# A diagonal of reciprocal roots in place of scaling and transposes, in the norm ahead of a feed-forward part

## The chip, the cores and the metric

The kernel runs on one core of a Trainium2 chip. The time is that of one execution on the device, in microseconds (us); what is given for a kernel is the median of its runs. Each engine has a queue of its own, which it works through in order, and waits in it for semaphores: TensorE (PE, with PEld for its weight loads), VectorE (DVE), ScalarE (ACT), GpSimd (POOL) and SyncE (SP), which only issues DMAs here.

## What is computed

One layer of a latent generator, with 1024 positions of 1024 channels in fp32 (and 256 context positions, which end before the part that matters here): a modulated norm, an input projection, three mixing groups (Fourier, attention, gated DeltaNet), an output projection with a gate, and a feed-forward part with squared ReLU. The change lies in the second norm, between the two residual additions:

```python
def _rms(x, g):
    xf = x.astype(jnp.float32)
    y = xf * lax.rsqrt(jnp.mean(xf * xf, axis=-1, keepdims=True) + EPS)
    return (y * g.astype(jnp.float32)).astype(x.dtype)
...
    x = x + g1 * _mix_out(P, o_att, o_dn, lp['w_out'], lp['o_norm'])
    x = x + g2 * _mlp(_rms(x, lp['norm2']) * (1 + sc2) + sh2, lp['w_ff1'], lp['w_ff2'])
```

The feed-forward products contract over channels, so the normed rows are needed transposed, with channels on the partitions. There a channel's `norm2 * (1 + sc2)` and `sh2` are one number for each partition.

## The kernel before

The whole program is unrolled, and every tile of 128x128 or 128x512 is an instruction of its own. A scheduler sets the order on each engine when the program is built, by a model of how long instructions take and by priorities: code under `tc.high_priority(n)` is preferred by n places. So a change of a few lines can shift instructions of other code too. In what follows "L1480" is line 1480.

Products of fp32 accuracy are made by three products each, of high and low parts: `mm3` (L235 to L238) multiplies high by high, high by low and low by high, in the type fp32r. `mm` (L233) is a single product, in the type of its operands; with plain fp32 operands it is an fp32 product. `tp` (L241) is a transpose on PE, a product with the identity in transpose mode. All three write to PSUM banks (`ba`, `bk`). `act` (L220) is an ACT operation, so all ACT work carries that line. `split` (L1488 to L1490) cuts a tile into a high part (a cast, by ACT or DVE) and a low part (a subtraction, by DVE or POOL).

In front of the change stands the output projection (L1528 to L1554): four passes over 256 output columns, in each eight row tiles q. A tile's product goes through DVE (L1544, times the gate) and POOL (L1545, added to `ACC[q]`, the residual row tile of 128 x 1024). In the last pass `ACC[q]` is complete, and under the priority OFN = 1000 follow:

- `rms_ff(q)` (L1470): ACT squares the row tile with a running sum (two instructions that write `bk_78`), POOL works out the mean (L1474, L1475) and the reciprocal root (L1476, a power), one number for each row;
- a store of the row tile to DRAM (L1549), needed later for the second residual addition;
- after q = 3, `h2_first` (L1492): the first half, rows 0 to 511. `norm_ff(0)` (L1478 to L1480) scales four row tiles by their roots on DVE, 128 x 1024 each. Then for each block k of 128 channels `h2_T` (L1482) makes four transposes into one bank of a ring of three (`bk_76`, `bk_77`, `bk_79`), and ACT evicts the bank with the scale and the shift of that block's channels. DVE casts the high part (L1489); the low part goes to POOL for odd k and to DVE for even k.

The second half, rows 512 to 1023, is scaled with `norm_ff(1)` (priority OFN2 = 0) into the same four tiles ACC[0] to ACC[3], and `h2_second` (L1575, priority OFN3 = 400) makes the same transposes and evictions. It also needs differences with the first half: `joined` (L1580) puts the first half's high and low parts back together in a bank by two products with an identity (L1582, L233), and DVE subtracts (L1576). The feed-forward's first product is a Strassen-Winograd scheme of seven products (named 11, 12, s1, s2, s4, s3, 22), so it takes sums and differences of weights as well: `w1_prep` (L1517) makes the weights' sums on POOL (L1523, 128 x 512) in a ring `shr` of three buffers, which the first half's blocks use too; ACT casts the high part, DVE subtracts the low part (L1490). `ff1` (L1605) runs the products.

Buffers: `g1r` are the two buffers of the output projection's gate, `mrowb` two of the modulation rows, 256 columns each; `slot` are the 16 half tiles of `ACC`, reused after the norm for `t1`, `tr_` and the ring `ur` of the feed-forward's results.

Of the kernel before, what the change touches and what calls it, by code (L numbers as in the profile page):

```python
# [14 lines left out]
ALU = mybir.AluOpType  # L15
AX = mybir.AxisListType

P = 128
# [173 lines left out]
def body(tc, t, out):  # L192
# [3 lines left out]
    with ctx:  # L196
# [14 lines left out]
        V, G, T, Y, SC = nc.vector, nc.gpsimd, nc.tensor, nc.sync, nc.scalar  # L211
# [20 lines left out]
        def mm(o, l, r, start, stop):  # L232
            pe(T.matmul(o, l, r, start=start, stop=stop))  # L233
# [6 lines left out]
        def tp(o, i):  # L240
            pe(T.transpose(o, i, C["ident"]))  # L241
# [7 lines left out]
        C = {k: cstb[a >= 256]()[:, a % 256 if a < 256 else a - 256 : b if a < 256 else b - 256] for k, (a, b) in CST.items()}  # L249
# [3 lines left out]
        mrowb = [buf(256) for _ in range(2)]  # L253
# [1216 lines left out]
        def rms_ff(q):  # L1470
# [4 lines left out]
            G.tensor_scalar(st[:, 0:1], st[:, 0:1], 1.0 / D, EPS, op0=ALU.mult, op1=ALU.add)  # L1475
            G.tensor_tensor(st[:, 1:2], st[:, 0:1], neghalf[:, 0:1], op=ALU.pow)  # L1476

        def norm_ff(half):  # L1478
            for n in range(half * 4, half * 4 + 4):
                V.tensor_scalar(ACC[n - half * 4][:, :], ACC[n][:, :], rsb[n]()[:, 1:2], None, op0=ALU.mult)  # L1480

        def h2_T(k, hf):  # L1482
            b = tr2.next()
            for q in range(4):
                tp(b[:, q * P : (q + 1) * P], ACC[q][:, k * P : (k + 1) * P])
            act(hf, b, AF.Identity, scale=a2()[:, k : k + 1], bias=s2()[:, k : k + 1])

        def split(i, hi, lo, eng, heng=None):  # L1488
# [3 lines left out]
        def h2_first():  # L1492
            norm_ff(0)
            for k in range(KT):
                hf = shr.next()()
                h2_T(k, hf)
                hb = B11 if k < 4 else B21
                split(hf, hb[0]()[:, k % 4], hb[1]()[:, k % 4], G if k % 2 else V, V.tensor_copy)

# [57 lines left out]
            b.free()  # L1557
        with tc.high_priority(OFN2):
            norm_ff(1)
        for b in g1r + otb + catF + catD:  # L1560
            b.free()


# [6 lines left out]
            hpc += [x for pr_ in prs for x in pr_]  # L1570
            HB[nm] = [(x(), y()) for x, y in prs]
        slot = [view(b, z * 512, 512) for b in accb for z in range(2)]
        ur = Ring(slot[14:16] + slot[0:8:2] + slot[1:8:2] + slot[8:14])

        def h2_second():  # L1575
            sub = lambda o, i, x: V.tensor_tensor(o, i, x, op=ALU.subtract)  # L1576
            t1, tr_ = [x() for x in slot[8:12]], Ring([x() for x in slot[12:14]])

            def joined(nm, k):
                b = tr2.next()  # L1580
                for z in range(2):
                    mm(b, idb(), HB[nm][k][z], z == 0, z == 1)  # L1582
                return b

            for k in range(4):
                h2_T(k, t1[k])
                sub(t1[k], t1[k], joined("11", k))
                split(t1[k], *HB["t1"][k], V)
            for k in range(4):
                h22 = tr_.next()  # L1590
                h2_T(k + 4, h22)
# [65 lines left out]

        with tc.high_priority(OFN3):
            h2_second()
        ORDER = ("11", "12", "s1", "s2", "s4", "s3", "22")  # L1660
        for j in range(2):
            for nm in ORDER[0:2]:
# [161 lines left out]
```

## Time and profile before

| | us |
|---|---|
| median of 3 runs | 1450.36 |
| lowest and highest run | 1446.81, 1450.94 |
| the profiled execution, its own time | 1444.78 |
| its span, first to last instruction | 1443.0 |

What lies around the span is 1.78 us. The core's mean granted clock in the profiled execution was 0.985 of full speed.

In the profile a line of a timeline gives the start and length of instructions of one kind in a row, the engine, the source line, operation, tiles and shapes, their number, and in brackets the engine's idle time in front and what ended it. A line of the windows gives, for each engine, the busy time in that stretch of the span and the number of instructions; PEclk is TensorE's granted clock as a share of full speed. A group's line gives after the bar its busy time in us and the mean of one in ns, and after the second bar idle time in front of it. Tile names leave the buffer's number out: `bk` is any of the `bk_` banks, `fbase` any fp32 buffer of a large pool, `rbase` any fp32r buffer, `z1c` and `z2b` buffers of two more pools.

### The profile page before, as it was taken

What the parts mean: (1) busy time and instruction counts of PE and PEld (TensorE: products, weight loads), DVE (VectorE), ACT (ScalarE), POOL (GpSimd) and SP (SyncE); (2) the same over time, 40 slices, a digit from 0 to 9 for tenths busy, and PEclk for the clock granted to TensorE, in tenths of its full rate; (3) what the DMA queues carried; (4) which work ended last, traced back from release to release, by engine and by line L of the source; (5) the groups of instructions that cost most, each with busy time, mean ns of one, the idle gap of its engine ahead of it and who ended that gap; (6) DMA issues with size and microseconds to landing.
All of it is one profiled execution on the core that took longest, in us unless ns stands there. A gap on an engine that the chain in (4) does not pass through costs nothing.

```text
span 1443.0 us, 28992 instructions
## 1 busy us (share of the span) xinstructions
PE 1384.1 (96%) x11462; PEld 1116.0 (77%) x11462; DVE 987.1 (68%) x1697; ACT 703.4 (49%) x1239; POOL 645.7 (45%) x749
## 2 busy tenths in 40 slices
PE   5899989999999999989899899999999999999997
PEld 1677988867777777777799677888888888888886
DVE  0774679966778777787533987655556676776884
ACT  1742423235777777777313755555455543433331
POOL 2663667763546464484433634434443000000872
PEclk8999999989999999999999999999999999999999
DMA  9873133260000010142322225444446998766641
GB/s 330 327 253 125 45 99 80 63 154 17 9 25 10 10 40 2 37 138 66 105 91 107 84 81 174 162 148 151 135 137 225 323 387 261 237 233 218 197 154 59
DMA packets 143832, 198.46 MB, mean 138 GB/s; under 512 B 51549, under 2 KB 86991, under 8 KB 143439
## 3 DMA queue, kind: packets, MB, share of 16 engines
q1 hardware_dynamic: 142992, 195.91, 41.5%
q8 instruction: 90, 1.47, 0.4%
q10 hardware_dynamic: 703, 0.69, 0.1%
q14 instruction: 47, 0.39, 0.1%
HBM read 150.62 MB, written 45.94 MB: 136 GB/s over the span
## 4 chain that ended last, share of the span: by engine, by line
PE 48%; DVE 3%; DMA 2%; POOL 2%; issue 1%; ACT 0%; SPq 0%; DVEq 0%; POOLq 0%; ACTq 0%
PE bk L237 8%; PE bk L238 8%; PE bk L236 8%; PE ba L236 7%; PE ba L237 7%; PE ba L238 7%; PE bk L233 1%; DMA fbase<-la 1%; DMA la<-fbase 0%; DVE z1b L1355 0%; DMA fbase<-w_out 0%; POOL rbase L1490 0%; DMA fbase<-x 0%; PE bk L241 0%; DVE rbase L1018 0%
## 5 line engine op out<-in xcount | busy, mean ns | idle before, releaser
L220 ACT ACTIVATE rbase<-fbase 128x512 fp32r<-128x512 f32 (+3 forms) x255 | 171.4, 685 | 86.3 <-PE bk L237 55.7
L220 ACT ACTIVATE fbase<-bk 128x512 f32<-128x512 f32 (+3 forms) x224 | 124.9, 561 | 150.6 <-PE bk L233 94.1
L233 PE MATMUL bk<-rbase 128*128 128x256 f32 (+2 forms) x984 | 172.9, 310 | 4.4 <-ACT fbase L220 2.5
L233 PEld LDWEIGHTS bk<-rbase 128*128 128x128 f32 (+1 forms) x984 | 131.7, 174 | 34.1 <-ACT fbase L220 3.3
L220 ACT ACTIVATE z1c<-fbase 128x512 fp32r<-128x512 f32 (+1 forms) x120 | 76.7, 653 | 139.1 <-DMA fbase<-w_ff 53.3
L233 PE MATMUL ba<-rbase 128*65 128x512 f32 (+4 forms) x576 | 138.2, 342 | 5.6 <-DVE rbase L1018 4.3
L1523 POOL TENSOR_TENSOR fbase<-fbase 128x512 f32<-128x512 f32 x64 | 87.4, 1366 | 114.7 <-DVE z1c L1490 89.8
L220 ACT ACTIVATE fbase<-fbase 128x512 f32<-128x512 f32 (+4 forms) x148 | 96.0, 659 | 83.7 <-POOL fbase L1646 27.2
L1728 POOL TENSOR_TENSOR z2c<-z2c,fbase 128x512 f32<-128x512 f32 x16 | 31.1, 1967 | 204.5 <-ACT z2c L220 128.6
L994 DVE TENSOR_REDUCE fbase<-ba 128x1 f32<-128x512 f32 (+1 forms) x192 | 106.4, 594 | 21.3 <-PE ba L233 20.1
L220 ACT ACTIVATE rbase<-z1d 128x1024 fp32r<-128x1024 f32 x61 | 63.0, 1054 | 101.4 <-PE bk L237 86.8
L1490 DVE TENSOR_TENSOR z1c<-fbase,z1c 128x512 fp32r<-128x512 f32 x112 | 91.7, 823 | 24.2 <-ACT z1c L220 20.4
L1490 DVE TENSOR_TENSOR rbase<-z1d,rbase 128x1024 fp32r<-128x1024 f32 x61 | 84.9, 1408 | 32.0 <-ACT rbase L220 31.9
L1018 POOL TENSOR_TENSOR rbase<-fbase,rbase 128x512 fp32r<-128x512 f32 x56 | 72.1, 1287 | 67.5 <-ACT rbase L220 60.0
L236 PE MATMUL bk<-rbase 128*128 128x512 f32 x256 | 99.6, 389 | 0.0
L237 PE MATMUL bk<-rbase 128*128 128x512 f32 x256 | 99.6, 389 | 0.0
L238 PE MATMUL bk<-rbase 128*128 128x512 f32 x256 | 99.6, 389 | 0.0
L1018 DVE TENSOR_TENSOR rbase<-fbase,rbase 128x512 fp32r<-128x512 f32 x104 | 80.1, 770 | 24.4 <-ACT rbase L220 24.0
L1490 DVE TENSOR_TENSOR rbase<-fbase,rbase 128x1024 fp32r<-128x1024 f32 (+1 forms) x65 | 81.1, 1266 | 21.9 <-ACT rbase L220 21.6
L233 PEld LDWEIGHTS ba<-rbase 128*65 128x65 f32 (+1 forms) x576 | 76.1, 154 | 23.6 <-DVE rbase L1018 5.4
L237 PE MATMUL ba<-rbase 128*128 128x512 f32 x192 | 74.7, 389 | 0.0
L238 PE MATMUL ba<-rbase 128*128 128x512 f32 x192 | 74.7, 389 | 0.0
(350 smaller groups left out, 3773.1 us busy)
## 6 DMA issues: line engine op xcount, KB each, us to landing
fbase<-w_ff SPq DMA_DIRECT2D x70, 512.0 KB
u<-fbase SPq DMA_DIRECT2D x112, 256.0 KB
z2a<-w_mod SPq DMA_DIRECT2D x36, 512.0 KB
z1d<-w_ff SPq DMA_DIRECT2D x34, 512.0 KB
z1d<-u SPq DMA_DIRECT2D x33, 512.0 KB
fbase<-u SPq DMA_DIRECT2D x23, 512.0 KB
fbase<-w_in SPq DMA_DIRECT2D x16, 512.0 KB
fbase<-x SPq DMA_DIRECT2D x14, 512.0 KB
```

The source lines that it names most:

```text
L220: return SC.activation(o, i, f, **k)
L233: pe(T.matmul(o, l, r, start=start, stop=stop))
L236: pe(T.matmul(o, lh, rh, start=start, stop=False))
L237: pe(T.matmul(o, lh, rl, start=False, stop=False))
L238: pe(T.matmul(o, ll, rh, start=False, stop=stop))
L994: V.tensor_reduce(st4[:, z : z + 1], b, AX.X, ALU.max)
L1018: (G if k2 in GP and not any(a <= n < b for a, b in NGP) else V).tensor_tensor(hl[:, :, 1], p, f32(hl[:, :, 0]), op=ALU.subtract)
L1490: eng.tensor_tensor(lo, i, f32(hi), op=ALU.subtract)
L1523: G.tensor_tensor(w[nm], w[a], w[b], op=op)
L1728: G.tensor_tensor(c, c, G2[cs_.start // 512], op=ALU.mult)
```

## The change

Four views of 128 x 128 are cut out of `g1r[0]` and `mrowb[0]`. `norm_ff` no longer scales row tiles: it writes, for each row tile, the identity times the column of reciprocal roots, a diagonal matrix. `h2_T` no longer transposes: it multiplies the untouched slice of `ACC` (as the operand that is held, so that it comes out transposed) by that diagonal, in one fp32 product. So transposing and scaling are one operation. The row tiles are no longer overwritten, and the second half is read where it lies. `g1r` is released after `h2_second` instead of before it, and the slots of `t1`, `tr_` and `ur` change, since ACC[4] to ACC[7] now stay in use longer.

```diff
+        dgb = [view(b, z * P, P) for b in (g1r[0], mrowb[0]) for z in range(2)]
+
         def norm_ff(half):
             for n in range(half * 4, half * 4 + 4):
-                V.tensor_scalar(ACC[n - half * 4][:, :], ACC[n][:, :], rsb[n]()[:, 1:2], None, op0=ALU.mult)
-
-        def h2_T(k, hf):
+                V.tensor_scalar(dgb[n % 4](), C["ident"], rsb[n]()[:, 1:2], None, op0=ALU.mult)
+
+        def h2_T(half, k, hf):
             b = tr2.next()
             for q in range(4):
-                tp(b[:, q * P : (q + 1) * P], ACC[q][:, k * P : (k + 1) * P])
+                mm(b[:, q * P : (q + 1) * P], ACC[half * 4 + q][:, k * P : (k + 1) * P], dgb[q](), True, True)
             act(hf, b, AF.Identity, scale=a2()[:, k : k + 1], bias=s2()[:, k : k + 1])
...
-        for b in g1r + otb + catF + catD:
+        for b in otb + catF + catD:
             b.free()
...
-        ur = Ring(slot[14:16] + slot[0:8:2] + slot[1:8:2] + slot[8:14])
+        ur = Ring(slot[6:16] + slot[0:6])
...
-            t1, tr_ = [x() for x in slot[8:12]], Ring([x() for x in slot[12:14]])
+            t1, tr_ = [x() for x in slot[0:4]], Ring([x() for x in slot[4:6]])
...
         with tc.high_priority(OFN3):
             h2_second()
+        for b in g1r:
+            b.free()
```

The calls of `h2_T` pass the half. From `norm_ff` on, the changed kernel's lines are two higher than before's: POOL's weight sum is L1525 there, the low part's subtraction L1492, the subtractions of the second half L1578, the scaling L1482; the products stand on L233 and no longer on L241.

The scheduler also puts other instructions elsewhere. On ACT, at the change from the first half to the second, the last evictions of the first half read `bk_76` and `bk_77`, the `z1c` rows are casts of weights, and the first row that reads `bk_79` behind them evicts block 0 of the second half. In before:

```order
L220 ACTIVATE fbase<-bk_76,fbase 128x512
L220 ACTIVATE fbase<-bk_77,fbase 128x512
L220 ACTIVATE z1c<-fbase 128x512
L220 ACTIVATE fbase<-ba_73 128x512
L220 ACTIVATE z1c<-fbase 128x512 x3
L220 ACTIVATE fbase<-bk_79,fbase 128x512
```

And in the changed kernel, from the last eviction of `bk_77` on:

```order
L220 ACTIVATE fbase<-bk_77,fbase 128x512
L220 ACTIVATE z1c<-fbase 128x512 x2
L220 ACTIVATE bk_78,fbase<-fbase 128x512
L220 ACTIVATE fbase<-ba_73 128x512
L220 ACTIVATE z1c<-fbase 128x512 x3
L220 ACTIVATE fbase<-fbase 128x512 x2
L220 ACTIVATE z1c<-fbase 128x512 x3
L220 ACTIVATE fbase<-bk_79,fbase 128x512
```

Four casts stand ahead of that eviction in before, eight in the changed kernel, and the last three of them moved there past it.

On POOL, the last reciprocal roots (L1474 to L1476) lie among sums of weights and low parts of the first half. In before:

```order
L1474 TENSOR_TENSOR fbase<-fbase 128x1
L1523 TENSOR_TENSOR fbase<-fbase 128x512
L1475 TENSOR_SCALAR fbase<-fbase 128x1
L1490 TENSOR_TENSOR rbase<-fbase,rbase 128x512
L1476 TENSOR_TENSOR fbase<-fbase 128x1
L1523 TENSOR_TENSOR fbase<-fbase 128x512 x7
```

And in the changed kernel, where the last root is the last L1476:

```order
L1475 TENSOR_SCALAR fbase<-fbase 128x1
L1525 TENSOR_TENSOR fbase<-fbase 128x512
L1476 TENSOR_TENSOR fbase<-fbase 128x1
L1492 TENSOR_TENSOR rbase<-fbase,rbase 128x512
L1547 TENSOR_TENSOR fbase<-fbase 128x256
L1525 TENSOR_TENSOR fbase<-fbase 128x512
L1474 TENSOR_TENSOR fbase<-fbase 128x1
L1525 TENSOR_TENSOR fbase<-fbase 128x512
L1475 TENSOR_SCALAR fbase<-fbase 128x1
L1525 TENSOR_TENSOR fbase<-fbase 128x512
L1476 TENSOR_TENSOR fbase<-fbase 128x1
L1525 TENSOR_TENSOR fbase<-fbase 128x512 x3
```

Of the eight sums one stands ahead of the last root in before, and five do in the changed kernel; three are left behind it.

On DVE, where the second half's first subtractions (reading a `bk_` bank) begin, `z1c` rows are low parts of weight sums and `z2b` rows low parts of the second half. In before:

```order
L1480 TENSOR_SCALAR fbase<-fbase 128x1024
L1490 TENSOR_TENSOR z1c<-fbase,z1c 128x512 x2
L1631 TENSOR_TENSOR fbase<-ba_74,fbase 128x512
L1490 TENSOR_TENSOR z1c<-fbase,z1c 128x512
L1576 TENSOR_TENSOR fbase<-fbase,bk_76 128x512
L1576 TENSOR_TENSOR fbase<-fbase,bk_79 128x512
L1490 TENSOR_TENSOR z1c<-fbase,z1c 128x512
L1490 TENSOR_TENSOR z2b<-fbase,z2b 128x512
L1490 TENSOR_TENSOR z1c<-fbase,z1c 128x512
```

And in the changed kernel:

```order
L1492 TENSOR_TENSOR z1c<-fbase,z1c 128x512 x3
L1633 TENSOR_TENSOR fbase<-ba_74,fbase 128x512
L1482 TENSOR_SCALAR fbase<-fbase 128x128
L1492 TENSOR_TENSOR z1c<-fbase,z1c 128x512 x3
L1578 TENSOR_TENSOR fbase<-fbase,bk_76 128x512
L1578 TENSOR_TENSOR fbase<-fbase,bk_79 128x512
L1492 TENSOR_TENSOR z2b<-fbase,z2b 128x512 x2
```

The low parts of weight sums that lay between and behind the first subtractions now lie ahead of them, so that from the first subtraction to the second row of L1638 (L1640 in the changed kernel) DVE has 32 instructions where it had 35.

More of the change, by code (lines that the diff above doesn't have):

```diff
@@ L1495, in h2_first @@
                 hf = shr.next()()
-                h2_T(k, hf)
+                h2_T(0, k, hf)
                 hb = B11 if k < 4 else B21
@@ L1585, in h2_second @@
             for k in range(4):
-                h2_T(k, t1[k])
+                h2_T(1, k, t1[k])
                 sub(t1[k], t1[k], joined("11", k))
@@ L1590, in h2_second @@
                 h22 = tr_.next()
-                h2_T(k + 4, h22)
+                h2_T(1, k + 4, h22)
                 sub(t1[k], h22, t1[k])
```

## The prediction

> **What bounds the kernel now.** I read the profile page first, for the busy shares.
>
> ```profile
> span 1443.0 us, 28992 instructions
> PE 1384.1 (96%) x11462; PEld 1116.0 (77%) x11462; DVE 987.1 (68%) x1697; ACT 703.4 (49%) x1239; POOL 645.7 (45%) x749
> ```
>
> TensorE (PE) is busy for 96% of the span, so the change is read from the stretch in which its instructions run. Next came the busy time of each engine by windows, from the end of the output projection to the end of the feed-forward products.
>
> ```profile
> core 0: us, PE busy (x) PEld busy (x) DVE busy (x) ACT busy (x) POOL busy (x), PEclk, DMA share, GB/s
> 770.00:800.00 30.00, 30.00 (x246) 29.14 (x245) 17.39 (x28) 17.26 (x39) 16.48 (x30) 1.00 0.39 148
> 800.00:805.00 5.00, 5.00 (x23) 4.00 (x23) 4.33 (x5) 2.07 (x4) 4.83 (x6) 1.00 0.52 170
> 805.00:810.00 5.00, 4.19 (x21) 3.08 (x21) 4.37 (x4) 0.74 (x2) 4.83 (x6) 1.00 0.00 0
> 810.00:815.00 5.00, 2.67 (x11) 1.57 (x11) 3.96 (x4) 3.82 (x7) 4.15 (x4) 1.00 0.01 3
> 815.00:820.00 5.00, 4.20 (x15) 3.45 (x16) 4.96 (x6) 5.00 (x10) 4.71 (x3) 0.66 0.26 72
> 820.00:825.00 5.00, 3.81 (x23) 2.69 (x22) 5.00 (x9) 4.80 (x9) 0.00 (x0) 1.00 0.56 190
> 825.00:840.00 15.00, 15.00 (x66) 12.03 (x65) 13.03 (x23) 9.84 (x18) 0.00 (x0) 1.00 0.05 18
> 840.00:850.00 10.00, 9.43 (x39) 6.76 (x38) 8.86 (x16) 4.99 (x9) 3.27 (x2) 1.00 0.18 55
> 850.00:1425.00 575.00, 575.00 (x2508) 469.53 (x2507) 388.37 (x426) 261.71 (x369) 185.60 (x119) 1.00 0.60 201
> ```
>
> From 770 to 805 PE never idles; from 805 to 850 it idles 0.81 + 2.33 + 0.80 + 1.19 + 0.57 = 5.7 us; from 850 to 1425 again not at all. Work added to PE in the first or last of these stretches is paid in full; work added in the middle one can replace waiting. The waits of PE between 800 and 850 name the causes (in us, times, longest):
>
> ```profile
> PE bk L241 <- DVE fbase L1576: 2.6, 3, 1.4
> PE bk L233 <- ACT fbase L220: 1.8, 1, 1.8
> PE bk L241 <- DVE fbase L1480: 0.8, 1, 0.8
> PE ba L236 <- DVE fbase L1638: 0.6, 1, 0.6
> ```
>
> Only one wait, 0.8 us, is for the scaling (L1480) that the change replaces. The rest is for the eviction of the first block of the second half (L220) and for the subtractions behind it (L1576). PE's timeline shows where each falls:
>
> ```profile
> 798.25 0.60 PE L241 MATMUL bk<-fbase 128*128 128x128 f32 x4
> 809.86 0.44 PE L241 MATMUL bk<-fbase 128*128 128x128 f32 x2 [0.81 <-DVE fbase L1480]
> 811.54 0.40 PE L238 MATMUL bk<-rbase,z1c 128*128 128x512 f32 x1
> 813.69 0.73 PE L233 MATMUL bk<-rbase 128*128 128x512 f32 x2 [1.76 <-ACT fbase L220]
> 815.80 1.01 PE L241 MATMUL bk<-fbase 128*128 128x128 f32 x4 [1.38 <-DVE fbase L1576]
> 820.99 0.66 PE L241 MATMUL bk<-fbase 128*128 128x128 f32 x4 [0.55 <-DVE fbase L1576]
> 823.38 0.66 PE L241 MATMUL bk<-fbase 128*128 128x128 f32 x4 [0.64 <-DVE fbase L1576]
> ```
>
> Behind the two long waits the granted clock falls: 0.66 on average from 815 to 820, which costs 5 x 0.34 = 1.7 us. The record's modelled end runs over its neighbour's start: four transposes last 0.60, but take 0.44 from start to start (0.11 each), so each gap is about 0.16 longer than the profile says, 1.0 us over six gaps. All that PE loses here is 5.7 + 1.7 + 1.0 = 8.4 us.
>
> **The change part by part.** *Products for transposes.* The change turns 64 transposes (8 blocks k x 4 row tiles x 2 halves) into 64 fp32 products of 128 columns. Before has no such product; the nearest are fp32 products of 256 columns, and of 40 and 80.
>
> ```profile
> 623.95 1.03 PE L233 MATMUL bk<-fbase,z1b 128*128 128x256 f32 x4
> 132.72 1.46 PE L233 MATMUL bk<-fbase 128*128 128x40 f32 x12
> ```
>
> An fp32 product leaves two records (the program issues six for these twelve). At 256 columns records follow each other every (1.03 - 0.38)/3 = 0.216 us (0.38 is a single record's length, so 1.03 - 0.38 are the three steps), at 40 and 80 columns every (1.46 - 0.27)/11 = 0.108. So a product of 128 columns costs between 2 x 0.108 and 2 x 0.216. I take 0.22: half of 256 columns at the same rate is 0.108, and the short records show the same floor. Against 0.11 for a transpose that is +0.11 each, 64 x 0.11 = +7.0 us of PE work: 3.5 in the first half, paid in full; 0.9 for blocks 0 and 1 of the second half, which PE does ahead of its long wait; 2.6 for blocks 2 to 7, where PE waits for DVE anyway. With the upper row it would be 64 x (0.43 - 0.11) = +20.6.
>
> The Trainium skill's page TensorE: Matmul & The Clock Gate, in its terms (xbus), says that transpose mode is four times faster for FP32. By that rule a product takes 4 x 0.11 = 0.44 and the sum is about +21, an estimate; the short records' 0.108 speaks for twice, not four times.
>
> *The scaling.* On DVE eight scalings of 128x1024 go and eight of 128x128 come.
>
> ```profile
> L1480 DVE TENSOR_SCALAR fbase<-fbase x8: 742/837/1766, 781.1 to 808.0; 128x1024 f32<-128x1024 f32 x8
> L933 DVE TENSOR_SCALAR rbase<-fbase x2: 218/221/224, 4.5 to 237.9; 128x136 fp32r<-128x136 f32 x2
> 808.04 1.77 DVE L1480 TENSOR_SCALAR fbase<-fbase 128x1024 f32<-128x1024 f32 x1 [0.44 <-POOL fbase L1476]
> ```
>
> A small one is bounded by 0.22 (128x136) and 0.84 (the old median); I take 0.22. The last old one ran 1.77 us, in front of the last transposes. PE's wait of 0.81 for it goes: PE now comes there later, by the first half's 3.5 us, and the last small scaling is over sooner. That the second half is read where it lies, not copied, costs nothing and frees nothing that PE waits for. The later release of two gate buffers and the new slots (t1, tr_, ur) change no wait in the trace: from 850 on PE is never idle, and that full queue is the cover. Without it a late slot would cost the length of the operation that frees it, some 0.7.
>
> *What is late next.* The eviction of block 0 of the second half. In before it stands on ACT behind four casts of weights, in the new order behind eight, and the last of these needs the last of POOL's eight weight sums (the pieces of ACT and POOL above). Since ACT works its queue in turn, all evictions of the second half queue behind that sum, and with them DVE's subtractions and PE's joined products.
>
> ```profile
> 812.34 0.63 ACT L220 ACTIVATE z1c<-fbase 128x512 fp32r<-128x512 f32 x1 [0.72 <-POOL fbase L1523]
> 812.88 0.76 ACT L220 ACTIVATE fbase<-bk,fbase 128x512 f32<-128x512 f32 x1
> 803.21 1.81 POOL L1523 TENSOR_TENSOR fbase<-fbase 128x512 f32<-128x512 f32 x1
> 807.02 0.99 POOL L1476 TENSOR_TENSOR fbase<-fbase 128x1 f32<-128x1 f32 x1
> 807.98 4.33 POOL L1523 TENSOR_TENSOR fbase<-fbase 128x512 f32<-128x512 f32 x3
> 813.00 6.78 POOL L1523 TENSOR_TENSOR fbase<-fbase 128x512 f32<-128x512 f32 x4 [0.69 <-DVE z1c L1490]
> L1523 POOL TENSOR_TENSOR fbase<-fbase 128x512 f32<-128x512 f32 x8 | 12.7, 1597 | 0.9 <-DVE z1c L1490 0.7
> L1490 POOL TENSOR_TENSOR rbase<-fbase,rbase 128x512 fp32r<-128x512 f32 x4 | 6.2, 1553 | 2.1 <-DVE rbase L1489 2.0
> ```
>
> In before the eighth sum ends at 813.00 + 6.78 = 819.8. POOL's work is the same in the new order, five sums now stand ahead of the last reciprocal root (L1476), one in before. It can end sooner by the 0.9 + 2.1 us that POOL waits for DVE, which loses its long scalings, and by what slows sums beside DVE (8 x 1.6 = 12.7 against 8 x 1.44 = 11.5 at the pace of the row at 807.98): 1.2. So between 819.8 - 4.2 = 815.6 and 819.8. I take 817.0, nearer to the early end, because POOL is nearly without idle time already but DVE's load falls. One cast (0.6) and the eviction (0.8) later, at 818.4, the joined product may start: 4.7 us after the 813.69 of before. PE itself is there at 811.54 + 0.40 - 0.81 + 3.5 + 0.9 = 815.5, so it waits 2.9 instead of 1.76.
>
> *What is given back.* The stretch behind it, to the last of the waits above, is DVE's: 4.96 and 5.00 of 5 us busy from 815 to 825. In the new order 32 DVE instructions stand there, 35 before; three lo-subtractions of weights (L1490) went ahead (the piece of DVE above). Such an instruction costs
>
> ```profile
> 816.27 0.68 DVE L1490 TENSOR_TENSOR z1c<-fbase,z1c 128x512 fp32r<-128x512 f32 x1
> 818.56 1.77 DVE L1490 TENSOR_TENSOR z1c<-fbase,z1c 128x512 fp32r<-128x512 f32 x1
> ```
>
> 0.68 alone and up to 1.77 beside POOL. Three cost 2.0 to 3.2 with at most one at the long price; I take 2.5. The 2.6 us of products lie under DVE there. Sum: +4.7 - 2.5 = **+2.2 us**, with ends at 0 (sum at 815.6 and 3.2 given back: +3.3 - 3.2) and +4.3.
>
> The clock stays in the sum as before: one stretch of 0.66 behind a long wait. The Trainium skill's page TensorE: Matmul & The Clock Gate, in Part 4 on the PE-mode transpose, says that transposes do not count as PE-busy in the same way for the clock. By that rule products would hold the clock where transposes let it fall, and the sum would be +0.5 instead of +2.2; no run yet shows it, and the row shows the low clock behind idle time.
>
> The profiled run took 1444.78 us, 5.6 below the median of the three runs (1450.36). I add the 2.2 to the median: 1452.6.
>
> **The rivals.**
>
> *Slower: the price is paid in full.* Place: ACT's eviction of block 0 behind POOL's last sum. It decides when that sum ends after 819.1: then the joined product starts after 820.5, 6.8 late, less 2.5, over 4.3. If nothing is recovered the time is 7.0 more, 1457.4; if the longer wait brings another half-clock stretch, 7.0 + 1.7 = +8.7, 1459.1. For it: POOL is over 4.1 of 5 us busy in every window from 800 to 820. Against it: POOL's 2.1 us of waits for casts, which should shrink. Chance 0.30.
>
> *The waits all go.* 7.0 - 8.4 = -1.4, 1449.0: PE, later by its own work, finds everything ready. For it: DVE loses some 6 us of long scalings (8 x (0.84 to 1.77 less 0.22)). Against it: the eviction stands in a later place on ACT. Chance 0.10.
>
> *Products cost as in the upper row*, 0.43 each: 1450.36 + 20.6 = 1471.0. Against it: the short records. Chance 0.03.
>
> *The change does not cost what it says:* a 128-column product goes as fast as a transpose, and PE's 5.7 us of idle time goes: 1444.7. Against it: two records for each product. Chance 0.05.
>
> **How the numbers follow.** The forecast has what is left, 0.52, with its own range of 1450.4 to 1454.7. About 0.3% (4.35 us) is what a measurement of this kernel can tell from no change. Faster by more: only the last rival, 0.05. Within it: the forecast and the case without waits, 0.52 + 0.10 = 0.62. Slower: 0.30 + 0.03 = 0.33. The range goes from the case without waits, less 1 us for a median whose three runs spread over 4 (1448.0), to the slower rival's end (1459.1); it leaves out 0.08.
>
> **What would show each step.** In the profile of the changed kernel: 128 records of L233 with 128 columns, 0.11 us apart, and PE without idle time to about 808; no wait of PE for the scaling; POOL's last sum of this batch ending near 817; block 0's eviction near 818, with a wait of 2 to 4 us on PE for ACT before the joined product; fewer and shorter waits for L1576 behind it; the same pace from 850 on. I am wrong if records lie 0.2 apart, if the eviction comes before 815 (then the waits go and the time does not rise), if it comes after 820, or if PE idles anywhere after 850.

## The result and the profile after

| | before | changed |
|---|---|---|
| median, us (4 runs each) | 1449.65 | 1459.58 |
| lowest and highest run | 1446.81, 1450.94 | 1458.82, 1460.12 |
| ratio to before, 95% interval | | 1.0079 [1.0064, 1.0094] |
| the profiled execution, its span | 1444.78, 1443.0 | 1459.2, 1457.4 |

The changed kernel is slower by 9.9 us by the medians, half a microsecond beyond the end of the range. The page says that PE still bounds it, with 12.9 us more busy time in a span that is 14.4 us longer:

```profile
span 1457.4 us, 29120 instructions
PE 1397.0 (96%) x11526; PEld 1129.9 (78%) x11526; DVE 990.2 (68%) x1697; ACT 704.3 (48%) x1239; POOL 645.0 (44%) x749
```

Not all of the 14.4 us is the change's. The groups of the projection's gate products on DVE (the row gives number, shortest, median and longest in ns, then the start of the first and the last in us) show how far each execution was before it came to anything that the change touches. In before:

```profile
L1544 DVE TENSOR_TENSOR fbase<-ba,fbase x23: 416/424/425, 709.0 to 797.8; 128x256 f32<-128x256 f32 x23
```

In the changed kernel, two lines further down:

```profile
L1546 DVE TENSOR_TENSOR fbase<-ba,fbase x23: 412/424/426, 713.7 to 809.4; 128x256 f32<-128x256 f32 x23
```

The first gate product starts 4.7 us later, the last one 11.6. So the profiled execution of before was early by 4.7 us (its own time, 1444.78 us, lies below the four runs of the table), and what the change does begins in between: 11.6 - 4.7 = 6.9 us by the last row tile of the projection. From here on times are also counted from the first gate product, 709.0 and 713.7: to the end it is 1443.0 - 709.0 = 734.0 us in before and 1457.4 - 713.7 = 743.7 in the changed kernel, +9.7, close to the 9.9 of the medians. The last reciprocal root starts at 98.1 in before (807.02 in the prediction's rows) and at 104.8 in the changed kernel, 6.7 later.

The windows of the changed kernel, where in before PE idled from 805 to 825:

```profile
810.00:815.00 5.00, 4.74 (x25) 3.71 (x24) 3.60 (x3) 1.84 (x4) 5.00 (x5) 1.00 0.24 85
815.00:820.00 5.00, 5.00 (x23) 3.85 (x21) 3.97 (x4) 2.15 (x4) 4.84 (x7) 1.00 0.33 102
820.00:825.00 5.00, 0.90 (x5) 0.52 (x4) 3.18 (x3) 2.04 (x4) 3.68 (x3) 1.00 0.28 91
825.00:830.00 5.00, 3.65 (x13) 3.23 (x14) 3.36 (x5) 3.23 (x6) 0.00 (x0) 0.54 0.55 171
830.00:835.00 5.00, 5.00 (x29) 4.60 (x29) 1.98 (x3) 2.81 (x5) 0.00 (x0) 0.78 0.00 0
840.00:850.00 10.00, 10.00 (x45) 8.01 (x44) 8.98 (x15) 6.74 (x13) 0.00 (x0) 1.00 0.09 31
850.00:860.00 10.00, 7.88 (x35) 6.05 (x34) 9.27 (x14) 4.98 (x9) 1.61 (x1) 1.00 0.17 53
```

PE works until it stands still for almost all of 820 to 825; then the granted clock is low for two windows. Its waits there:

```profile
PE bk L233 <- ACT fbase L220: 4.7, 1, 4.7
PE bk L236 <- DVE fbase L1578: 2.1, 1, 2.1
PE bk L233 <- DVE fbase L1482: 1.0, 2, 0.7
```

The wait for ACT has grown from 1.8 to 4.7 us; the others make 3.1 us together, where before had 4.0. The timeline of PE shows the price of a product and where the waits fall:

```profile
798.74 2.84 PE L233 MATMUL bk<-fbase 128*128 128x128 f32 x24
...
812.94 0.71 PE L233 MATMUL bk<-fbase 128*128 128x128 f32 x4 [0.26 <-DVE fbase L1482]
820.89 0.71 PE L233 MATMUL bk<-fbase 128*128 128x128 f32 x4 [0.70 <-DVE fbase L1482]
826.35 2.07 PE L233 MATMUL bk<-rbase 128*128 128x512 f32 x4 [4.74 <-ACT fbase L220]
828.22 1.91 PE L233 MATMUL bk<-fbase 128*128 128x128 f32 x8
```

The group L233 of 128 columns has 128 records for the 64 products, and 24 of them in a row take 2.84 us, one every 0.112 (the last one's length of 0.27 taken off). The row at 820.89 has the products of the second half's blocks 0 and 1 that need the last root: they start 107.2 us after the first gate product, where the transposes that need it (809.86 in the prediction's rows) stood at 100.9 in before. ACT and POOL show what the joined product then waits for:

```profile
820.94 0.61 ACT L220 ACTIVATE z1c<-fbase 128x512 fp32r<-128x512 f32 x1
824.48 1.15 ACT L220 ACTIVATE z1c<-fbase 128x512 fp32r<-128x512 f32 x2 [2.92 <-POOL fbase L1525]
825.53 1.43 ACT L220 ACTIVATE fbase<-bk,fbase 128x512 f32<-128x512 f32 x2
```

```profile
812.76 0.72 POOL L1547 TENSOR_TENSOR fbase<-fbase 128x256 f32<-128x256 f32 x1
...
818.52 0.99 POOL L1476 TENSOR_TENSOR fbase<-fbase 128x1 f32<-128x1 f32 x1
819.48 1.28 POOL L1525 TENSOR_TENSOR fbase<-fbase 128x512 f32<-128x512 f32 x1
821.52 2.93 POOL L1525 TENSOR_TENSOR fbase<-fbase 128x512 f32<-128x512 f32 x2 [0.76 <-DVE z1c L1492]
```

The evictions of blocks 0 and 1 (825.53) stand behind two casts, and those behind POOL's last sum, which ends at 824.45. PE's row at 826.35 has the joined products, which write banks of the same ring and wait for the first of these evictions.

PE's account over this stretch: the products cost 64 x (0.224 - 0.11) = 7.3 us more; idle time is 4.7 + 2.1 + 1.0 = 7.8 in place of 5.7, +2.1; the low clock takes 3.65 x 0.46 + 5.00 x 0.22 = 2.8 us of busy time in place of 4.20 x 0.34 = 1.4, +1.4; two gaps fewer, -0.3. The sum is 10.5 against the 9.7 of the two profiles; 0.8 stays unexplained (some records are missing, ends are modelled). Nothing of the price was covered by waits, as the prediction's slower rival had it; that rival let the waits stay as they were, and here they grew.

### The profile page after: what moved, and what is told of

Same layout as the page of the kernel before. It is cut to its first block, busy times and chain, and to the rows that moved or that the text cites. A ratio compares the mean times of both kernels' runs of the same rounds, so it can differ in the third digit from the quotient of the medians.

```text
span 1457.4 us, 29120 instructions
## 1 busy us (share of the span) xinstructions
PE 1397.0 (96%) x11526; PEld 1129.9 (78%) x11526; DVE 990.2 (68%) x1697; ACT 704.3 (48%) x1239; POOL 645.0 (44%) x749
## 5 line engine op out<-in xcount | busy, mean ns | idle before, releaser
L220 ACT ACTIVATE rbase<-fbase 128x512 fp32r<-128x512 f32 (+3 forms) x255 | 171.5, 685 | 88.2 <-PE bk L237 58.5
L233 PE MATMUL bk<-rbase 128*128 128x256 f32 (+2 forms) x984 | 173.5, 312 | 7.3 <-ACT fbase L220 5.5
L233 PEld LDWEIGHTS bk<-rbase 128*128 128x128 f32 (+1 forms) x984 | 132.9, 175 | 36.9 <-ACT fbase L220 6.7
L233 PE MATMUL ba<-rbase 128*65 128x512 f32 (+4 forms) x576 | 140.2, 346 | 5.0 <-DVE rbase L1018 3.5
L1525 POOL TENSOR_TENSOR fbase<-fbase 128x512 f32<-128x512 f32 x64 | 86.0, 1345 | 119.2 <-DVE z1c L1492 89.6
L1492 DVE TENSOR_TENSOR z1c<-fbase,z1c 128x512 fp32r<-128x512 f32 x112 | 91.4, 820 | 25.6 <-ACT z1c L220 21.2
L1492 DVE TENSOR_TENSOR rbase<-z1d,rbase 128x1024 fp32r<-128x1024 f32 x61 | 85.3, 1412 | 29.3 <-ACT rbase L220 29.2
L233 PEld LDWEIGHTS ba<-rbase 128*65 128x65 f32 (+1 forms) x576 | 77.3, 157 | 23.2 <-DVE rbase L1018 4.6
L1492 DVE TENSOR_TENSOR rbase<-fbase,rbase 128x1024 fp32r<-128x1024 f32 (+1 forms) x65 | 81.5, 1273 | 16.5 <-ACT rbase L220 14.4
```

Of the source, the lines that this page charges most:

```text
L220: return SC.activation(o, i, f, **k)
L1492: eng.tensor_tensor(lo, i, f32(hi), op=ALU.subtract)
L1525: G.tensor_tensor(w[nm], w[a], w[b], op=op)
```

## The experiments

Two explanations were open. *Late root:* products ahead of the projection's last tile push that tile, with it the last root, the products of the second half that need it and their eviction, and so the waits that should have covered the price move along with it; then the loss depends on where the products stand. *Plain price:* PE is the bound and pays for every product wherever it stands. Times over before in this table come from the ratios, in us of 1448:

| run | ratio, 95% interval | over before |
|---|---|---|
| changed kernel | 1.0079 [1.0064, 1.0094] | +11.4 |
| before again | 0.9998 [0.9985, 1.0012] | -0.3 |
| first half only | 1.0049 [1.0034, 1.0064] | +7.1 |
| second half only | 1.0037 [1.0024, 1.0051] | +5.4 |
| products with the identity | 1.0085 [1.0069, 1.0101] | +12.3 |
| projection first, products | 1.0019 [1.0006, 1.0031] | +2.8 |
| projection first, transposes | 1.0019 [1.0007, 1.0032] | +2.8 |
| slots alone | 1.0002 [0.9990, 1.0014] | +0.3 |
| casts on POOL, products | 1.0044 [1.0028, 1.0060] | +6.4 |
| last tiles first, products | 1.0049 [1.0034, 1.0065] | +7.1 |
| last tiles first, transposes | 1.0043 [1.0030, 1.0056] | +6.2 |
| casts on POOL, transposes | 0.9996 [0.9985, 1.0008] | -0.6 |
| projection first and casts on POOL, products | 1.0024 [1.0013, 1.0036] | +3.5 |

**Before again.** Nothing is edited.

> Nothing is edited: a second profile of the kernel before. In the two profiles the changed kernel already lies 4.7 us behind at 709 us (the gate product of the last but one passes, L1544), ahead of every instruction that the change touches. Theory: that is scatter between executions, so this profile takes 1446 to 1451 us, is late by 2 to 6 us at 709, and has the same idle time of PE between the last transposes of the first half and the start of the long busy stretch, 5 to 6.5 us. Rival: the change makes earlier stages slower; then this profile takes 1444 to 1446 us and lies within 1 us of the first one at 709.

The profiled execution took 1448.28 us, with a span of 1446.5. Its gate products:

```profile
L1544 DVE TENSOR_TENSOR fbase<-ba,fbase x23: 416/425/425, 712.1 to 801.4; 128x256 f32<-128x256 f32 x23
```

The first lies 3.1 us later than in the first profile, and 1446.5 - 712.1 = 734.4 us remain, where the first had 734.0; PE idles for 5.0 us against 5.7. So in these two profiles the stretch is the same to a few tenths and the time ahead of it is not: 3.1 of the 4.7 us by which the changed kernel was behind at this point come without any edit, and the runs below that leave the projection's earlier passes alone have the first gate product at 708.5 to 713.2 us.

What does differ within the stretch is how long the clock stays low. The second profile of before has

```profile
815.00:820.00 5.00, 1.96 (x8) 0.99 (x7) 5.00 (x7) 3.82 (x8) 4.15 (x4) 0.78 0.02 3
820.00:825.00 5.00, 5.00 (x19) 3.75 (x17) 4.96 (x5) 4.90 (x10) 3.38 (x2) 0.54 0.50 158
```

which is 1.96 x 0.22 + 5.00 x 0.46 = 2.7 us of lost clock, where the first had 1.4 and the changed kernel 2.8. So the +1.4 for the clock in the account above can't be put down to the change. Against this second profile the account is 7.3 for the products, 7.8 - 5.0 = 2.8 for idle time, 0.1 for the clock and -0.2 for one gap fewer, 10.0 in place of 9.3. Idle time and clock together cost some 3 us more either way (3.5 and 2.9).

**The first half alone.**

```diff
             for n in range(half * 4, half * 4 + 4):
-                V.tensor_scalar(ACC[n - half * 4][:, :], ACC[n][:, :], rsb[n]()[:, 1:2], None, op0=ALU.mult)
+                if half:
+                    V.tensor_scalar(ACC[n - 4][:, :], ACC[n][:, :], rsb[n]()[:, 1:2], None, op0=ALU.mult)
+                else:
+                    V.tensor_scalar(dgb[n](), C["ident"], rsb[n]()[:, 1:2], None, op0=ALU.mult)
...
-                tp(b[:, q * P : (q + 1) * P], ACC[q][:, k * P : (k + 1) * P])
+                if half:
+                    tp(b[:, q * P : (q + 1) * P], ACC[q][:, k * P : (k + 1) * P])
+                else:
+                    mm(b[:, q * P : (q + 1) * P], ACC[q][:, k * P : (k + 1) * P], dgb[q](), True, True)
```

> Only the first half is done by fp32 products with the diagonal; the second half is scaled and transposed as before. Theory (late root): the first half's products delay the output projection's last row tile on PE, with it the last reciprocal root on POOL, the last weight sums and the eviction of block 0 of the second half on ACT; nearly all of the loss is here: +6.5 to +10 us, the last root 5 to 7 us later than before. Rival (plain price): PE pays 32 x 0.114 = 3.6 us for the products and the order does not matter: +3 to +5 us. Rival (second half): the loss comes from the products of the second half, which run at the low clock: 0 to +2 us here.

+7.1 us [4.9, 9.3], twice the 3.6 us that 32 products cost. The gate products and PE's waits:

```profile
L1552 DVE TENSOR_TENSOR fbase<-ba,fbase x23: 410/425/426, 708.5 to 805.6; 128x256 f32<-128x256 f32 x23
```

```profile
PE bk L233 <- ACT fbase L220: 4.2, 1, 4.2
PE bk L241 <- DVE fbase L1483: 3.3, 2, 2.3
```

The last gate product comes 97.1 us after the first, where before has 88.8 and the second profile of before 89.3: 8 us late, and the waits for the second half's scaling (L1483 here) and for ACT grow from 2.6 to 7.5 us, though nothing in the second half is edited. All waits of PE together grow from 5.7 to 8.1 us. This is what the late root gave, and the plain price falls short.

**The second half alone.** The same switch the other way round, on top of the changed kernel's slots.

> Only the second half is done by products with the diagonal; the first half is scaled in place and transposed as before. The slots and the release of the gate buffers are those of the changed kernel. Theory (late root): the projection's last tile and the last root stay in time, so the waits of PE cover the products: -1 to +3 us. Rival (plain price): 32 x 0.114 = 3.6 us: +3 to +5. Rival (second half): +6 to +10.

+5.4 us [3.5, 7.4], more than the late root gave and a little above the plain price's +3 to +5; the profile, from the first gate product to the end, has 1451.3 - 712.7 = 738.6 us, +4.6. The last root is 0.8 to 1.2 us late by the same count. PE's waits come in other places than in before, and are as long, 5.4 us for 5.7:

```profile
PE bk L233 <- ACT fbase L220: 2.9, 1, 2.9
PE bk L236 <- DVE fbase L1584: 2.1, 1, 2.1
PE bk L233 <- DVE fbase L1483: 0.4, 1, 0.4
```

So the late root is not the whole: the second half's products have a cost of their own, and here, as the plain price has it, no wait covers it.

**Products with the identity.** Only the transposes are replaced; the order on the engines follows as in the changed kernel.

```diff
-                tp(b[:, q * P : (q + 1) * P], ACC[q][:, k * P : (k + 1) * P])
+                mm(b[:, q * P : (q + 1) * P], ACC[q][:, k * P : (k + 1) * P], C["ident"], True, True)
```

> The scaling on DVE stays as in the kernel before; only each transpose becomes an fp32 product with the identity, so the price of the products is alone. By the order its instructions stand as in the changed kernel (five weight sums ahead of the last root, eight casts ahead of the eviction of block 0). Theory (late root): the loss of the changed kernel or more, as DVE keeps its scalings: +9 to +13 us. Rival (plain price): 64 x 0.114 = +7.3 us, +6 to +9. Rival (something other than the products, such as slots or diagonals, brings the loss): below +5.

+12.3 us [10.0, 14.6], with the scaling kept. The products, with the order that the scheduler makes for them, bring the whole loss, and taking the large scalings off DVE, with all else in the change, is worth about 1 us, within the intervals nothing.

**Projection first.** The last column pass is given a priority over the first half, first in the changed kernel and then in before.

```diff
-                b = omr.next()[:, 0:256]
+                with tc.high_priority(2000 if n4 == 3 else 0):
+                    b = omr.next()[:, 0:256]
...
-                    with tc.high_priority(OFN):
-                        rms_ff(q)
+                    with tc.high_priority(2000):
+                        rms_ff(q)
+                    with tc.high_priority(OFN):
```

> The changed kernel, with the last column pass of the output projection and its root mean squares given a priority of 2000, above the first half's 1000: by the order 8 of the first half's 32 products stand ahead of the projection's last product where 32 did, no weight sum ahead of the last root where five did, and two casts ahead of the eviction of block 0 of the second half where eight did. All 64 products stay. Theory (late root): the last root comes 5 us or more earlier than in the changed kernel, PE's wait for ACT before the joined products shrinks to under 2.5 us, and the time is +2 to +6 us over before. Rival (plain price): wherever the products stand, they are paid: +8 to +12 us, as in the changed kernel. Rival (low clock): only the half-clock stretch counts; then the time falls by its 1.5 to 3 us alone.

> The kernel before with the same priority, as the control for the run with the projection first: by the order 12 of the first half's transposes stand ahead of the projection's last product where 32 did, and two weight sums ahead of the last root. Theory (late root): the root comes earlier here too, the scaling's wait of 0.8 us goes and the wait for the eviction may go: -4 to 0 us. Rival (plain price): PE's work is unchanged and so is the time: -1 to +1. If the order as such loses, because the first half is late: +1 to +4.

(In before 24 transposes stood ahead of the projection's last product; the 32 named for the control is the changed kernel's number.) Both took 1.0019 of before, each with an interval of 1.8 us to either side. The first gate product comes at 719.7 and 721.4 us, where the runs above have 708.5 to 713.7. Probably the priority of 0 that this edit puts on the other three passes moved work ahead of the projection; it is nearly alike in both. Products for transposes cost 0.0 us here by the ratios, 1.4 by the medians (1452.51 and 1451.15), where they cost 11.4 in the scheduler's own placing. The two orders are alike, not the same: 8 products stand ahead of the projection's last one in the first, 12 transposes in the second. With products the last root starts 86.8 us after the first gate product, where the changed kernel has 104.8, and PE's waits are

```profile
PE bk L233 <- DVE fbase L1580: 1.8, 1, 1.8
PE bk L237 <- DVE z2b L1492: 0.5, 1, 0.5
PE ba L236 <- DVE fbase L1642: 0.2, 1, 0.2
```

and in the control with transposes

```profile
PE bk L233 <- ACT fbase L220: 2.0, 1, 2.0
PE bk L241 <- DVE fbase L1480: 1.6, 1, 1.6
PE bk L241 <- DVE fbase L1578: 1.1, 1, 1.1
PE ba L237 <- POOL rbase L1490: 0.9, 1, 0.9
PE ba L236 <- DVE fbase L1640: 0.6, 1, 0.6
PE bk L237 <- DVE z2b L1490: 0.5, 2, 0.3
```

2.5 us against 6.7: of the 7.3 us of products 4.2 are paid out of waits. The low clock took 1.5 us against 2.4, but two profiles of before differ by more than that, so it is not counted. From the first gate product to the end the two profiles have 731.4 and 730.1 us, 1.3 apart. This rejects the plain price: by it the pair had to lie 7.3 us apart. The control itself missed what the late root gave for it (-4 to 0) and came where an order that loses as such was put (+1 to +4): this placing loses 2.8 us for transposes.

**Slots alone.** Transposes and scaling as before, in place, on the new slots, with the late release.

> Transposes and scaling stay; only the buffers are those of the changed kernel: the second half is scaled in place and transposed from there, t1, tr_ and ur use the new slots, and the gate buffers are released later. Theory (late root) and rival (plain price): no part of the loss, -1.5 to +1.5 us. Rival (slots): the loss that the second half's run left above its 3.6 us of products is here, +1.5 to +3 us, and a wait of PE over 1 us stands some 138 us behind the first gate product of the projection, as in the second half's run.

+0.3 us [-1.4, +2.0]: no part of the loss that ten runs can tell, and the wait of 2.1 us in the second half's run does not come from the slots. The profile of this run is longer than its ratio says, 1449.9 - 712.5 = 737.4 us from the first gate product to the end. Of the 3.4 us above before 1.5 are a low clock ahead of the norm (3.05 x 0.12 + 5.00 x 0.22, from 717 to 727). PE's wait for ACT is 3.7 us here, though the time hardly rises: a longer wait alone does not show a loss.

**Casts on POOL.** The first eight sums' high parts are cast by POOL.

```diff
-                split(w[nm], h, l, V)
+                split(w[nm], h, l, V, G.tensor_copy if nm in SUMS and j < 2 else None)
```

> The changed kernel, but the high parts of the first eight weight sums are cast by POOL itself in place of ACT, so that no cast that waits for a sum stands ahead of the eviction of block 0 of the second half. Theory (late root, and on top the casts): the eviction comes as soon as its products are done, some 4 us earlier behind them, and the wait of 4.7 us on PE for it goes; DVE's subtraction for block 0 still stands behind six low parts of weights. So -1 to -4 us against the changed kernel if the products' lead counts, 0 to +2 if DVE's queue or POOL's longer work takes its place. Rival (plain price): no change against the changed kernel, within 1 us.

> The kernel before, with the high parts of the first eight weight sums cast by POOL in place of ACT: no cast stands ahead of the eviction of block 0 of the second half, where four did. Theory (late root, and the casts on top): in before the eviction lies some 3 us behind its transposes, 1.8 of which PE waits for; that wait goes and the time falls by 1 to 3 us. Rival (plain price of PE's work): PE's work is the same, within 1 us of before. If POOL's longer sums and DVE's low parts take its place: +1 to +3.

In the changed kernel it takes back 5 us of 11.4 by the ratios, a little more than the 1 to 4 expected. There the eviction of block 0 starts 108.9 us after the first gate product where the changed kernel has 111.8, and PE's wait for ACT is 0.6. The three rows:

```profile
PE bk L233 <- DVE fbase L1482: 2.4, 1, 2.4
PE bk L236 <- DVE fbase L1578: 2.1, 1, 2.1
PE bk L233 <- ACT fbase L220: 0.6, 1, 0.6
```

So the casts in ACT's queue are part of the chain. What is left starts with the wait for the last diagonal (L1482), whose root is no earlier than in the changed kernel (106.7 and 104.8). In before the same edit changes nothing within its interval, -0.6 us: the wait for ACT falls from 1.8 to 0.9, and others (L1490, low parts) take its place. The expected 1 to 3 us did not come; this is what the plain price gave. Between the two runs the products cost 7.0 us, nearly their whole price: with the late root left in, the waits do not cover them.

**Last tiles first.** The priority only for row tiles 4 to 7, with no statement ahead of them touched.

```diff
-                b = omr.next()[:, 0:256]
+                with tc.high_priority(1200) if n4 == 3 and q >= 4 else ExitStack():
+                    b = omr.next()[:, 0:256]
...
-                    with tc.high_priority(OFN):
+                    with tc.high_priority(1200 if q >= 4 else OFN):
                         rms_ff(q)
+                    with tc.high_priority(OFN):
```

> As the run with the projection first, but the priority (1200) is given only to row tiles 4 to 7 of the projection's last column pass, and no statement ahead of them is touched, so that the order on every engine is the changed kernel's up to the last pass: it removes from that run the earlier reordering, by which the first gate product came some 7 us later. By the order 8 of the first half's products stand ahead of the projection's last product, no weight sum ahead of the last root and two casts ahead of the eviction of block 0. Theory (late root): the waits of PE cover the products; 729 to 734 us from the first gate product of the projection to the end where the changed kernel had 743.7 and before 734.2, -4 to +1 us in time. Rival (plain price): 741 to 745, +7 to +11. Rival (a scatter or gain of the earlier reordering): 734 to 739, +1 to +5.

> The kernel before with the same priority on the last four row tiles, control for the run with the last tiles first: no weight sum ahead of the last root and three casts ahead of the eviction of block 0. Theory (late root): the scaling and the eviction still make PE wait about as long as in the earlier control (6.7 us there), 729 to 733 us from the first gate product to the end, -5 to 0 us in time, and the changed kernel with the same priority within 2 us of it. Rival (plain price): the changed kernel is 7 us or more behind this one.

(By the order 9 products stand ahead of the projection's last one in the first of the two, not 8.) Both missed the number: +7.1 and +6.2, where I had expected a gain. Taken by itself the first lies where the plain price put it (+7 to +11); it is the control that speaks against the plain price, which wanted the two 7 us apart. The last root is in time (98.9 after the first gate product in both, 98.1 in before), but the eighth weight sum now ends at 117.4 and 116.9 where it ended at 110.8, and evictions of the second half stand on ACT behind casts of these sums: the chain's other end has become the late one. That this is all of the 6.2 us is not shown: PE's waits in the control are 8.9 us, 3.2 above before's. By the pair, products cost 0.9 us here by the ratios, and 2.4 by the profiles (742.3 and 739.9 us from the first gate product to the end). An early root alone thus does not help in this placing; that it would with early sums is argued, from the run with the projection first, where the eighth sum ends at 107.1.

**Both edits.** Projection first and casts on POOL, in the changed kernel.

> The changed kernel with the projection's last pass at priority 2000 and the casts of the first eight weight sums on POOL. With the projection first alone it took +2.7 us over before, with the casts on POOL alone +6.8 where the changed kernel is +10 to +11. Theory (late root and casts are two parts of one chain): with the root early the eviction waits for two casts only, so that the casts on POOL bring little here: +1.5 to +3.5 us over before. Rival (two separate costs that add): 2.7 - 3.5 = about -1 us.

+3.5 us [+1.9, +5.2]: no gain on top of the projection first. The two are parts of one chain, not costs that add. No version with products beats before here.

## Why the prediction was wrong, point by point

**The price of a product** was right: two records of 0.112 us, +0.114 each, +7.3 us in all where the prediction had 7.0.

**The scaling.** The prediction let the 0.8 us wait go and took 0.22 us for a small scaling. The group of the eight:

```profile
L1482 DVE TENSOR_SCALAR fbase<-fbase x8: 275/519/1309, 785.0 to 819.6; 128x128 f32<-128x128 f32 x8
```

The median is 0.519 us, and two waits for them remain, 1.0 us together. A small miss.

**"I take 817.0" for the end of POOL's last sum** is the step that failed first. It ended at 824.45, that is 824.45 - 4.7 = 819.7 on the clock of the profile before: where it ended there (819.8), at the late end of the bounds. The argument for the early end was that DVE's load falls, and the sums did run faster, 11.2 us for the eight against 12.7. But between the first and the last of them POOL now also has a residual addition (L1547, 0.72 us) and the root of one more row tile (1.70 us), and it waits for 1.7 us in place of 0.9, so that the batch took 17.7 us for 16.6 (806.80 to 824.45, and 803.21 to 819.78). The sum itself was thus not late; late was the eviction, which by its new place on ACT had to wait for it, and for two casts where the prediction had one: 111.8 us after the first gate product where it was 103.9. In the prediction's own terms, the joined product behind the eviction was to start 4.7 us later, and it started 826.35 - 4.7 - 813.69 = 8.0 later. The slower rival named this place and its threshold (819.1), and priced it at over 4.3 and up to 8.7.

**What the prediction did not see** is the late tile. It had shown that five weight sums now stand ahead of the last root but took the root itself for early, since PE "comes there later, by the first half's 3.5 us". The order has 32 products ahead of the projection's last product, where 24 transposes stood: 32 x 0.224 - 24 x 0.11 = 4.5 us more of PE's time. The projection's last product on PE, in before and in the changed kernel, agrees:

```profile
797.21 0.28 PE L238 MATMUL ba<-z1c,rbase 128*128 128x256 f32 x1
```

```profile
806.29 0.28 PE L238 MATMUL ba<-z1c,rbase 128*128 128x256 f32 x1
```

From the first gate product that is 88.2 and 92.6 us, 4.4 later. Then the tile's gate product has to wait its turn on DVE, behind high and low parts of the first half:

```profile
806.89 1.50 DVE L1491 CAST rbase<-fbase 128x512 fp32r<-128x512 f32 x1
...
809.37 0.42 DVE L1546 TENSOR_TENSOR fbase<-ba,fbase 128x256 f32<-128x256 f32 x1
```

It starts 2.8 us after PE's product ends, where in before it was 0.3 (797.80), and so that tile was 6.9 us late, the root 6.7, and the second half's products that need it 6.3. In the changed kernel itself PE waits only 1.0 us for diagonals, since its own work made it late too; the long wait is for the eviction. The run with the casts on POOL parts the two: without the casts ahead of it the eviction still came 5.0 us later than in before (108.9 and 103.9), behind the last diagonal, and the casts' place made that 7.9. The run with the first half alone shows the late tile without any other part of the change.

**"I take 2.5" for what is given back** failed as well, and by more. Behind the joined product 9.7 - 8.0 = 1.7 us were lost where 2.5 were to come back. The stretch was called DVE's, on the windows from 815 to 825. But the row from 825 to 840 had PE busy for 15.00 of 15, so there was little idle time to hide 24 products in; and in the changed kernel's windows from 825 to 835 DVE is busy for 3.36 + 1.98 = 5.3 of 10 us and PE for 8.65, at the low clock. There DVE was not the limit. Nor is the price of "0.68 alone" for a low part what its row shows: it starts at 816.27, in the middle of POOL's four sums (813.00 to 819.78). The run with the second half alone costs 5.4 us, though its root is nearly in time.

**The clock** was kept as before, one low stretch, and the changed kernel lost 2.8 us to it for the 1.4 of the first profile of before; the second profile of before lost 2.7, so the change is not shown to have made it longer. The rule that the prediction took from the Trainium skill's page TensorE: Matmul & The Clock Gate, Part 4 (transposes do not count as PE-busy in the same way), would have spared the low stretch with products; it did not go away here, and eight records that take 1.05 us at the full clock took 1.91 in it. The same page's four times for FP32, in its terms, is not what these rows show: twice 0.112 against 0.11.

**The likeliest case** thus had the right place on ACT and the wrong ends, three times on the hopeful side, and left the late tile out. What stays open: why the two placings that were tried cost 2.8 and 6.2 us with transposes too, and whether one exists that has root and sums early and costs nothing elsewhere. With the projection first and products, 1451.1 - 719.7 = 731.4 us remain from the first gate product, 2.6 less than in before; the loss lies ahead of it, where other work was moved. The changed kernel's own order with transposes in it was not tried, since the scheduler's order follows from the price; so its loss is split between the products' price and the longer waits by PE's account alone.

## What to carry to other kernels

When an engine that bounds a stage is given more work, find the last producer that this work is placed in front of, and follow its chain to the waits that are to cover the price: cover that depends on that producer moves along and covers nothing. Where a scheduler sets the order, an edit's cost is its price in the new order, so a control with the same priorities and the old operation helps to tell the price from the placing. And between two bounds with a queue in the middle, a value near the early end needs a reason for every instruction in that queue.

## What the runs showed of the hardware

A scaling of 128x128 on DVE took 0.275 us at best, but 1.30 and 1.21 us where POOL was at work. The two rows, and POOL's at the same time (one is at 819.48 above):

```profile
811.59 1.30 DVE L1482 TENSOR_SCALAR fbase<-fbase 128x128 f32<-128x128 f32 x1 [0.43 <-POOL fbase L1476]
...
819.63 1.21 DVE L1482 TENSOR_SCALAR fbase<-fbase 128x128 f32<-128x128 f32 x1
```

```profile
811.52 1.28 POOL L1492 TENSOR_TENSOR rbase<-fbase,rbase 128x512 fp32r<-128x512 f32 x1
```

Both end within 0.1 us of POOL's instruction (812.89 and 812.80, 820.84 and 820.76), as if DVE had waited for it: an eighth of the columns saved a quarter to a third of the old 1.77 us. The Trainium skill's page SBUF — State Buffer, section SBUF: two separate sides, states that the port pair that DVE and GpSimd share is locked for a whole instruction, by GpSimd or by a DVE instruction in a two-port mode or with two SBUF inputs, and that the other engine is blocked. These two rows agree; in which mode the scaling runs no run shows.

In the low clock PE's 128-column products took about twice as long (8 records 1.91 us at 828.22, against this row of the run with the projection first):

```profile
820.65 1.05 PE L233 MATMUL bk<-fbase 128*128 128x128 f32 x8
```

So a wait can cost more than its own length: the 4.7 us wait was followed by 2.8 us of lost clock. But the loss does not follow the length of the wait: behind the same waits before lost 1.4 us in one profile and 2.7 in the other, and behind the changed kernel's wait of 2.1 us the clock stayed at 1.00 (the window from 850 to 860).
